# A state-space layer inside a decoder trunk: order of its stages, form of its small products, and the queue of its tables

## Chip, cores and metric

The kernel runs on one core of a Trainium2 chip. The metric is device time in microseconds (us) of one execution. The core has five engines that each work through an instruction list of their own in order: PE (matrix products), DVE and ACT (elementwise work, ACT also functions such as Gelu), POOL (elementwise work), and SP, which here only issues DMAs. POOL and ACT issue DMAs too, each from its own place in its list. An engine waits where an operand is not there yet or a buffer is still in use.

## What is computed

The reference is one step of a decoder trunk of two layers on 512 prompt tokens and 64 sample tokens, D = 1024. Each layer is `x += mixer(rmsnorm(x)); x += swiglu(rmsnorm(x))`. Layer 0's mixer is a dilated attention with a KV cache, layer 1's is an S5 state-space layer. The change is in that layer and in the setup of its tables:

```python
u = h @ w_in                                  # 64 groups of 16 channels
abar = exp(lam * dt)                          # complex, 64 states for each group
bbar = ((abar - 1.0) / lam)[..., None] * bmat
# x_t = abar * x_{t-1} + bbar u_t ;  y_t = Re(C x_t) + d_skip * u_t
g = gelu(y)
z = g @ w_glu
val, gate = split(z, 2)
return val * sigmoid(gate), h_last
```

The sample tokens are 8 rows of 8 tokens that start from given states; the prompt starts from zero.

## The kernel before

**Trunk.** Features lie on the partitions: `xT` holds 8 blocks of 128 features by 576 tokens. A large product takes float32 weights apart into a high and a low part (`split_w`: ACT writes `whi` at L99, DVE the rest `wlo` at L100), activations likewise (`xgh`, `xgl`), and adds three products, high by high, low by high and high by low, in `mm6` (L108), 288 tokens each. `fetch_w` (L85) issues a weight load on SP and, paced by a rate (`RF` by default), now and then one of the copies that shift the KV cache. PE writes to three rotating PSUM buffers `acc` 0 to 2 and a single `aux`. The order of all instructions is laid out by a scheduler from the order of the calls and the dependences; each engine then keeps its list.

**Tables.** `ssm_setup` runs in pieces during FFN 0. For each feature block f = 0..7 (128 features, 8 groups) it computes four tables and stores them to DRAM scratch: W (input to states), E (powers of the decay, one store for all f, L1291), T (input to output inside a chunk of 8 tokens, L1355) and V (states to output, four stores of 128 KB, L1369). POOL computes V (L1361 to L1366) and multiplies gt by rstd for the FFN (L1029). At the end of setup the tables of f = 0..3 are loaded back on SP (`consts`, L1096 to L1102), those of f + 4 on ACT's queue after stage 3 of f. DVE's first operation after the E store, a memset of `cb` (L1298), uses the memory from which E was stored, so it waits for that store to land.

**The norm ahead of the layer.** While FFN 0 ends, `Norm.add` for each of 8 blocks makes xgh, xgl and, for all but the first, a square on ACT (L193, into one buffer `sq`) that POOL adds to `ssum` (L194). `finish` (L199) is the product that sums it over the partitions.

**The state-space stage** (`ssm_phase`). Tokens are grouped in 64 prompt chunks and 8 sample chunks of 8 tokens, 72 columns.
- stage 1, c = 0..3: the input product of two blocks f, times the norm (L1408, DVE), to DRAM and back as `U` (128 by 8 by 72; L1409, L1413 on SP).
- stage 2, f: S = W U, 16 products of 128 rows and 64 columns (L1423); ACT copies S to `Sb` (L1425); DVE runs the recurrence over chunks (L1438 to L1447, two scans) and writes the chunk states `Xt` (L1450, L1451). Before, `Xt` has real and imaginary parts on the two halves of the partitions and one of the two half-blocks gl per slice, so that four DVE operations of 64 partitions write it; `xs0`, the sample states in that layout, is built in setup by four POOL copies (L1252).
- stage 3, f: Y = T U + V X, for each of 8 column blocks one T product (L1461) and one V product (L1462) of 128 by 128 weights; both in full float32, two records each in the trace. Gelu on ACT (L1464), to DRAM and back in token order (`yt`), split to high and low: G[f]. Y is `aux` for even f, `acc0` for odd f.
- The GLU product in 4 column blocks takes all G[f], then `Norm.add` and FFN 1 follow.

Before, the calls run as: stage 1(0), 1(1), S(0), S(1), 1(2), S(2), S(3), 1(3), stage 3(0), 3(1), S(4), S(5), 3(2), 3(3), S(6), 3(4), S(7), 3(5), 3(6), 3(7), GLU, where the scheduler moves single products between neighbours.

## Time and profile before

| what | value |
|---|---|
| median of 3 timed runs | 1497.02 us (1496.78 to 1498.91) |
| profiled execution | 1499.43 us, span 1497.7 us |
| granted clock of PE | 0.998 |
| PE busy | 1472.2 us (98% of the span) |
| DVE, ACT, POOL busy | 895.8, 527.8, 323.1 us |

In a row of groups the columns are the line, engine and operation, the names out<-in, PE's form in rows*columns (a name such as 128*64 is a weight of 128 rows and 64 columns), the shape, the count, then busy time in us and the mean of one in ns, and the idle time just before with what ended it. A timeline row starts with the start in us and the length in us; `x2` is two instructions in one row, and a note in brackets is the idle time before it and what ended it. A row of waits has the total in us, the count, and the longest. In a DMA row the last number is the median time from issue to landing.

### The profile page before, as it was taken

How to read it: one execution, taken by the hardware profiler on the slowest of the kernel's cores; microseconds unless marked ns; L12 is line 12 of the kernel's file. 1: busy time of each engine (PE TensorE's matmuls, PEld its weight loads, DVE VectorE, ACT ScalarE, POOL GpSimd, SP SyncE). 2: the span in 40 equal slices, each digit the busy share in tenths (PEclk: the TensorE clock that was granted, in tenths of full speed). 3: DMA queues.
4: the chain of work that ended last, by engine and by line, in shares of the span. 5: the costliest groups of instructions: out<-in, count | busy, mean ns of one | idle time of the engine just before them, and what ended most of it. 6: DMA issues, size and time to landing. Idle time of an engine off the chain costs nothing. (4 is left out here: it accounts for less than half of the span.)

```text
span 1497.7 us, 29564 instructions
## 1 busy us (share of the span) xinstructions
PE 1472.2 (98%) x12406; PEld 1384.5 (92%) x12406; DVE 895.8 (60%) x1507; ACT 527.8 (35%) x814; POOL 323.1 (22%) x377
## 2 busy tenths in 40 slices
PE   9999999999999999999999999999999999999998
PEld 7888777777899999999999999899999999999998
DVE  5898988745569545388687768745443323333332
ACT  4534455465552211322223453433432212221222
POOL 2022231320030174134436520201111001100100
PEclk9999999999999999999999999999999999999999
DMA  7566788989875555677867668865555655442212
GB/s 248 209 234 229 237 278 270 365 295 348 247 252 191 204 212 204 245 238 282 288 203 246 221 219 262 232 217 168 186 197 196 223 195 195 137 138 85 83 56 81
DMA packets 191861, 322.64 MB, mean 215 GB/s; under 512 B 40016, under 2 KB 138128, under 8 KB 190320
## 3 DMA queue, kind: packets, MB, share of 16 engines
q1 hardware_dynamic: 183488, 303.24, 60.0%
q10 hardware_dynamic: 5072, 10.04, 2.0%
q0 software_dynamic: 3168, 7.48, 1.5%
q8 instruction: 97, 1.59, 0.4%
q14 instruction: 36, 0.29, 0.1%
HBM read 289.22 MB, written 118.78 MB: 272 GB/s over the span
## 5 line engine op out<-in xcount | busy, mean ns | idle before, releaser
L108 PE MATMUL acc<-xgh,wlo 128*128 128x288 f32 x1760 | 377.9, 296 | 2.2 <-DVE wlo L100 2.2
L108 PE MATMUL acc<-xgh,whi 128*128 128x288 f32 x1760 | 379.1, 297 | 0.1
L108 PE MATMUL acc<-xgl,whi 128*128 128x288 f32 x1760 | 377.7, 296 | 1.0 <-DVE xgl L174 1.0
L100 DVE TENSOR_TENSOR wlo<-raw,whi 128x1024 fp32r<-128x1024 f32 (+1 forms) x166 | 214.9, 1295 | 261.9 <-ACT whi L99 258.4
L99 ACT ACTIVATE whi<-raw 128x1024 fp32r<-128x1024 f32 (+1 forms) x166 | 172.4, 1038 | 476.2 <-PE acc L108 446.0
L108 PEld LDWEIGHTS acc<-xgh,wlo 128*128 128x128 f32 x1760 | 283.2, 188 | 2.7 <-DVE wlo L100 2.5
L108 PEld LDWEIGHTS acc<-xgl,whi 128*128 128x128 f32 x1760 | 283.1, 189 | 1.5 <-DVE xgl L174 1.3
L108 PEld LDWEIGHTS acc<-xgh,whi 128*128 128x128 f32 x1760 | 282.7, 189 | 1.5 <-issue 1.0
L1029 POOL TENSOR_TENSOR gt<-gt,rstd 128x576 f32<-128x576 f32 x44 | 72.9, 1659 | 489.3 <-ACT gt L1028 489.1
L108 PE MATMUL acc<-hh,wlo 128*128 128x288 f32 x704 | 150.8, 295 | 2.1 <-DVE wlo L100 2.1
L108 PE MATMUL acc<-hh,whi 128*128 128x288 f32 x704 | 151.6, 296 | 0.0
L108 PE MATMUL acc<-hl,whi 128*128 128x288 f32 x704 | 150.9, 295 | 0.0
L340 PE MATMUL acc<-whi,xh 128*128 128x512 f32 x288 | 118.8, 414 | 0.5 <-ACT xh L280 0.4
L108 PEld LDWEIGHTS acc<-hh,wlo 128*128 128x128 f32 x704 | 112.9, 188 | 2.3 <-DVE wlo L100 2.3
L108 PEld LDWEIGHTS acc<-hh,whi 128*128 128x128 f32 x704 | 113.0, 188 | 0.6 <-issue 0.6
L108 PEld LDWEIGHTS acc<-hl,whi 128*128 128x128 f32 x704 | 113.1, 188 | 0.0
L340 PE MATMUL acc<-wlo,xh 128*128 128x512 f32 x288 | 112.2, 391 | 0.0
L340 PE MATMUL acc<-whi,xl 128*128 128x512 f32 x288 | 111.5, 393 | 0.0
L1050 DVE TENSOR_TENSOR xT<-acc,xT 128x576 f32<-128x576 f32 x48 | 36.1, 756 | 53.5 <-PE acc L108 53.5
L194 POOL TENSOR_TENSOR ssum<-ssum,sq 128x576 f32<-128x576 f32 x21 | 36.8, 1753 | 136.2 <-ACT sq L193 106.9
L340 PEld LDWEIGHTS acc<-whi,xl 128*128 128x128 f32 x288 | 54.0, 188 | 12.0
L340 PEld LDWEIGHTS acc<-whi,xh 128*128 128x128 f32 x288 | 54.0, 188 | 11.2 <-ACT xh L280 0.9
(395 smaller groups left out, 2008.5 us busy)
## 6 DMA issues: line engine op xcount, KB each, us to landing
o_kv_s<-cache_kv_w SPq DMA_DIRECT2D x64, 1020.0 KB, 6.9
kc<-cache_kv_w SPq DMA_DIRECT2D x100, 512.0 KB, 7.4
raw<-ffn_w_gate SPq DMA_DIRECT2D x44, 512.0 KB, 3.9
raw<-ffn_w_up SPq DMA_DIRECT2D x44, 512.0 KB, 3.9
raw<-ffn_w_down SPq DMA_DIRECT2D x40, 512.0 KB, 3.5
raw<-w_qkv SPq DMA_DIRECT2D x36, 512.0 KB, 7.4
kc<-qscr SPq DMA_DIRECT2D x32, 512.0 KB, 6.7
o_kv_s<-cache_kv_w SPq DMA_DIRECT2D x16, 1008.0 KB, 6.4
```

Source lines behind the costliest of these rows:

```text
L99: s.activation(hi, raw, AF.Copy)
L100: mark[0] = v.tensor_tensor(lo, raw, hi.bitcast(F32), OP.subtract)
L108: pem[0] = te.matmul(ps[:, c, :HN], w, x[:, c * HN:(c + 1) * HN], start=first and i == 0, stop=last and i == 2)
L194: g.tensor_tensor(self.ss, self.ss, sq, OP.add)
L340: ins = nc.tensor.matmul(*a, **kw)
L1029: g.tensor_tensor(t, t, nin.r, OP.mult)
L1050: v.tensor_tensor(xv, ps[m][:, :, :HN], xv, OP.add)
```

## The change

1. **Order of the stages.** `stage1` takes a function that it calls between its two halves: S(1) lies inside stage 1(2), S(3) and stage 3(0) inside stage 1(3). Stage 3 of 6 and 7 moves into the first GLU column block, whose second half goes through the k blocks with the gate and the value product side by side. S(0) uses `acc1`, stage 3(7) `aux`.
2. **Form of the products.** A T product becomes two of 64 columns. The V table and `Xt` get the recurrence's layout, [128, ri, q, chunk] with gl on the partition halves; a V product of 128 by 128 becomes four of 64 by 64 (two ri, two column halves), which add in PSUM. `Xt` is written by two DVE operations on 128 partitions, has four buffers in place of three, and takes the sample states from `x0`; `xs0` and its copies go.
3. **Tables.** V is stored by one DMA for each f; the V and E stores and all table loads are issued by POOL. `consts_in` (W, E) of f + 4 follows stage 2 of f, `consts_out` (T, V) follows stage 3.
4. `RF` goes from 0.7 to 0.72, the GLU fetches issue no cache copies, and `uP` shares its three buffers with `yt`.

```diff
-RF = 0.7
+RF = 0.72
...
+    def consts_in(f, q):
...
         q.dma_start(Ec, scn["E"][f])
+        KC[f] = [Wc, Ec]
+
+    def consts_out(f, q):
...
-        Vc = kc.tile([128, 4, 2, 128], F32, name="Vc")
-        q.dma_start(Vc, scn["V"][f].rearrange("r p q l c -> (r p) q l c"))
+        Vc = kc.tile([128, 2, 4, 128], F32, name="Vc")
+        q.dma_start(Vc, scn["V"][f])
+        KC[f] += [Tc, Vc]
...
-            for ri in range(2):
-                for gl in range(2):
-                    g.tensor_copy(xs0[ri * 64:ri * 64 + 64, gl], x0[gl * 64:gl * 64 + 64, ri])
...
-            nc.sync.dma_start(scn["E"].rearrange("f p r q c -> p r f q c"), ee.rearrange("p r (f q) c -> p r f q c", f=8))
+            g.dma_start(scn["E"].rearrange("f p r q c -> p r f q c"), ee.rearrange("p r (f q) c -> p r f q c", f=8))
...
-                for gl in range(2):
-                    for ri in range(2):
-                        nc.sync.dma_start(scn["V"][f, ri, :, :, gl, :], vv[gl * 64:gl * 64 + 64, ri].rearrange("p q c t -> p q (c t)"))
+                g.dma_start(scn["V"][f], vv.rearrange("p r q c t -> p r q (c t)"))
                 yield
-        consts(0, nc.sync)
-        consts(1, nc.sync)
+        consts(0, g)
+        consts(1, g)
     kp.append(out["es"].enter_context(L["right"]("ssmk1", bufs=2)))
-    consts(2, nc.sync)
-    consts(3, nc.sync)
+    consts(2, g)
+    consts(3, g)
...
-        for gl in range(2):
-            hs = slice(gl * 64, gl * 64 + 64)
-            v.tensor_tensor(Xt[0:64, gl, :, 1:64], ra[hs, 0], ta[hs, 0], OP.subtract)
-            v.tensor_tensor(Xt[64:128, gl, :, 1:64], ra[hs, 1], ta[hs, 1], OP.add)
+        v.tensor_tensor(Xt[:, 0, :, 1:64], ra[:, 0], ta[:, 0], OP.subtract)
+        v.tensor_tensor(Xt[:, 1, :, 1:64], ra[:, 1], ta[:, 1], OP.add)
...
-        for gl in range(2):
-            for q in range(4):
-                o = Y[:, gl, q * 72:q * 72 + 72]
-                te.matmul(o, Tc[:, 2 * q + gl, :], U[:, 2 * q + gl, :], start=True, stop=False)
-                te.matmul(o, Vc[:, q, gl, :], X[f][:, gl, q, :], start=False, stop=True)
+        for q in range(4):
+            qc = slice(q * 72, q * 72 + 72)
+            for gl in range(2):
+                for h in range(0, 128, 64):
+                    te.matmul(Y[h:h + 64, gl, qc], Tc[:, 2 * q + gl, h:h + 64], U[:, 2 * q + gl, :], start=True, stop=False)
+            for ri in range(2):
+                for gl in range(2):
+                    gs = slice(gl * 64, gl * 64 + 64)
+                    for h in range(0, 128, 64):
+                        te.matmul(Y[h:h + 64, gl, qc], Vc[gs, ri, q, h:h + 64], X[f][gs, ri, q, :], start=False, stop=ri == 1)
...
-            consts(f + 4, s)
+            consts_out(f + 4, g)
...
-    stage2(1)
-    stage1(2)
+    stage1(2, lambda: stage2(1))
     stage2(2)
-    stage2(3)
     fetch2(D)
-    stage1(3)
-    stage3(0)
+    stage1(3, lambda: (stage2(3), stage3(0)))
     stage3(1)
+    stage2(4)
     fetch2(0)
-    stage2(4)
+    stage3(2)
     stage2(5)
-    stage3(2)
     stage3(3)
     stage2(6)
     stage3(4)
     stage2(7)
-    for f in range(5, 8):
-        stage3(f)
+    stage3(5)
...
     def glu_first():
-        pg, pv = [acc(1), acc(2)], [acc(0), aux.tile([128, 2, 512], F32, name="aux")]
-        for kh in range(2):
-            for ps, c0 in ((pg, D), (pv, 0)):
-                glu_half(ps, *split_w(W2[c0][kh]), kh)
+        pg = [acc(1), acc(2)]
+        glu_half(pg, *split_w(W2[D][0]), 0)
+        stage3(6)
+        wh, wl = split_w(W2[0][0])
+        pv = []
+        for m in range(2):
+            pv.append(aux.tile([128, 2, 512], F32, name="aux") if m else acc(0))
+            for k in range(4):
+                mm6(pv[m], wh[:, k, m * 128:(m + 1) * 128], wl[:, k, m * 128:(m + 1) * 128], *G[k], k == 0, False)
+            if m == 0:
+                stage3(7)
...
+        for k in range(4):
+            for ps, wh, wl in w:
+                for m in range(2):
+                    mm6(ps[m], wh[:, k, m * 128:(m + 1) * 128], wl[:, k, m * 128:(m + 1) * 128], *G[4 + k], False, k == 3)
```

The first place is PE's list in the middle of stage 3. Before, in the stretch after stage 3(1), T (L1461) and V (L1462) products of one form alternate, with S(4) (L1423) between two blocks:

```order
L1461 MATMUL acc_10986<-U,Tc 128x72
L1462 MATMUL acc_10986<-Xt,Vc 128x72
L1423 MATMUL acc_11024<-U,Wc 64x72 x16
L1461 MATMUL aux<-U,Tc 128x72
L1462 MATMUL aux<-Xt,Vc 128x72
```

In the changed kernel PE's list has, around the same S(4) (now L1426), T (L1465) in fours and V (L1470) in eights, after the last product of stage 1(3):

```order
L108 MATMUL acc_10771<-xgh,wlo 128x288 x2
L1426 MATMUL acc_11056<-U,Wc 64x72 x16
L1465 MATMUL aux<-U,Tc 64x72 x3
L1465 MATMUL acc_10994<-U,Tc 64x72 x4
L1470 MATMUL acc_10994<-Xt,Vc 64x72 x8
```

Every T and V product now writes 64 of the partitions; T has 128 rows and V 64, so the form changes at each border between the two.

The second place is POOL's list at the end of FFN 0. Before, it holds the end of V for f = 7 (L1361 to L1366) and the adds to ssum (L194):

```order
L1363 TENSOR_TENSOR st_9894<-st_9894,vt_9895 128x512
L194 TENSOR_TENSOR ssum_5394<-ssum_5394,sq_9917 128x576
L1365 TENSOR_TENSOR vt_9895<-Cr_5478,Ai_5458 128x512
L1366 TENSOR_TENSOR st_9894<-st_9894,vt_9895 128x512
L194 TENSOR_TENSOR ssum_5394<-ssum_5394,sq_10049 128x576
L194 TENSOR_TENSOR ssum_5394<-ssum_5394,sq_10057 128x576
```

Now the same stretch of POOL's list has the V store (L1370) and the loads of the tables of f = 2 and 3 (L1095 to L1105):

```order
L1369 TENSOR_TENSOR st_9838<-st_9838,vt_9839 128x512
L1370 DMA v_scr_5040<-st_9838 128x1024
L194 TENSOR_TENSOR ssum_5394<-ssum_5394,sq_9926 128x576
L1095 DMA Wc_9899<-w_scr_5039 128x1024
L1097 DMA Ec_9901<-e_scr_5042 128x512
L1103 DMA Tc_9903<-t_scr_5041 128x1024
L1105 DMA Vc_9905<-v_scr_5040 128x1024
L1095 DMA Wc_9907<-w_scr_5039 128x1024
L1097 DMA Ec_9909<-e_scr_5042 128x512
L1103 DMA Tc_9911<-t_scr_5041 128x1024
L1105 DMA Vc_9913<-v_scr_5040 128x1024
L194 TENSOR_TENSOR ssum_5394<-ssum_5394,sq_10022 128x576
```

Eight loads, which need the memory that V's store of f = 7 reads, now stand between the first and the second add, and the first add stands behind V.

The third place is POOL's list around the end of E (the last product of its powers, and the copy of the last column). Before:

```order
L1128 TENSOR_TENSOR et_6504<-ee,U_5473 128x256
L1129 TENSOR_TENSOR ee<-et_6503,et_6504 128x32x8
L1290 COPY E_5459<-ee 128x64
L1362 TENSOR_TENSOR vt<-Cn,Ai 128x512
L1029 TENSOR_TENSOR gt<-gt,rstd 128x576 x5
```

Now, with the E store (L1294) and two E loads in the same list:

```order
L1135 TENSOR_TENSOR et_6445<-ee,U_5472 128x256
L1136 TENSOR_TENSOR ee<-et_6444,et_6445 128x32x8
L1293 COPY E_5459<-ee 128x64
L1294 DMA e_scr<-ee 256x8x256
L1365 TENSOR_TENSOR vt<-Cn,Ai 128x512
L1097 DMA Ec<-e_scr 128x512 x2
L1029 TENSOR_TENSOR gt<-gt,rstd 128x576 x4
```

The store follows the copy of E's last column in POOL's list, and the two loads stand between V's first operation and the FFN's products.

50 lines of the change are left out of this document (28 added, 22 removed).

## The prediction

> **What bounds the kernel now.** I read the page's head first, then the windows by stage, then the waits of PE inside the state-space stage, and last the timeline rows of the products that the change rewrites.
>
> ```profile
> span 1497.7 us, 29564 instructions
> 480.00:860.00 380.00, 375.66 (x2907) 372.26 (x2906) 250.19 (x439) 99.66 (x110) 163.60 (x137) 1.00 0.68 231
> 895.00:985.00 90.00, 86.78 (x865) 84.31 (x864) 67.54 (x116) 37.51 (x84) 11.27 (x19) 1.00 0.82 245
> ```
>
> In the window rows the columns after the length are the busy times of PE, PE's weight loads, DVE, ACT and POOL, then the clock and the DMA share. 480 to 860 is FFN 0 with the table setup in its gaps, 895 to 985 is the stage that the change rewrites. PE is busy in 86.78 of the 90 us there, so waits alone can give back about 3 us; anything larger has to come from PE doing the same work in less time. DVE, with 67.54 us, is the next engine. The profiled execution took 1499.43 us (span 1497.7), 2.4 us above the median of the three timed runs, 1497.02. I work out a difference on the trace and apply it to the median. A measurement of this kernel tells about 0.2% from no change, which is 3.0 us.
>
> These are all of PE's waits from 895 to 992 us:
>
> ```profile
> PE acc L108 <- DVE xgl L174: 1.0, 1, 1.0
> PE aux L1461 <- ACT ys L1464: 0.9, 2, 0.7
> PE acc L1423 <- ACT Sb L1425: 0.8, 2, 0.5
> PE aux L1462 <- issue: 0.5, 1, 0.5
> ```
>
> They add up to 3.2 us, all of them around stage 3 and the start of the GLU product.
>
> **The products of stage 3.** The rows start with the instruction's start and its length.
>
> ```profile
> 927.34 0.39 PE L1462 MATMUL aux<-Xt,Vc 128*128 128x72 f32 x2
> 927.56 0.39 PE L1461 MATMUL aux<-U,Tc 128*128 128x72 f32 x2
> 927.78 0.39 PE L1462 MATMUL aux<-Xt,Vc 128*128 128x72 f32 x2
> 928.01 0.39 PE L1461 MATMUL aux<-U,Tc 128*128 128x72 f32 x2
> ```
>
> One 128x128 product (two records, x2) starts every 0.223 us ((928.01 - 927.34) / 3). A block f has 8 T and 8 V products: 16 x 0.223 = 3.57 us. The halved T products have the form that stage 2 has already, 128 rows by 64 columns:
>
> ```profile
> L1423 PE MATMUL acc<-U,Wc 128*64 128x72 f32 x256 | 9.8, 229 | 0.8 <-ACT Sb L1425 0.8
> 911.44 0.43 PE L108 MATMUL acc<-xgh,wlo 128*128 128x288 f32 x2
> 911.80 1.22 PE L1423 MATMUL acc<-U,Wc 128*64 128x72 f32 x32
> 912.95 0.53 PE L108 MATMUL acc<-xgh,whi 128*128 128x288 f32 x2
> 913.32 0.42 PE L108 MATMUL acc<-xgl,whi 128*128 128x288 f32 x2
> 913.58 0.43 PE L108 MATMUL acc<-xgh,wlo 128*128 128x288 f32 x2
> ```
>
> Stage 2's 16 products are 32 records; from the first start to the last end they take 1.22 us, less the last one's own 0.23 us that is 0.99, so about 1.02 us with one more step. The two column halves run side by side. Sixteen halved T products per f therefore cost 1.02 us. The 32 V products of 64 rows and 64 columns have no row in the trace; the nearest are the small products of layer 0:
>
> ```profile
> 310.65 1.06 PE L760 MATMUL Sd<-kc,Pz 128*32 128x128 f32 x32
> 311.64 0.66 PE L760 MATMUL S<-kT,att 64*32 64x256 f32 x16
> 312.23 0.72 PE L760 MATMUL S<-kT,qT 64*128 64x128 f32 x8
> 312.88 1.09 PE L760 MATMUL pt<-ident,sm 128*128 128x128 f32 x8
> L760 PE MATMUL S<-kT,att 64*32 64x256 f32 x240 | 9.9, 388 | 0.0
> ```
>
> Of the 16 records of form 64*32 the last starts 0.27 us after the first (0.66 less the mean 0.388). Stage 2's step for a pair is 1.02/16 = 0.064 us at 72 columns, 0.23 us scaled to 256. So only one further group fits behind the first: eight run at once, which is both row halves and four column quarters. By that, four 64x64 products run at once: 8 groups of 2 records, 16 x 0.064 = 1.02 us per f. If the row halves did not overlap it would be 2.04. I take 1.02; the 64*32 rows have the row split in question.
>
> So T and V of one f go from 3.57 to 2.04 us, and eight of them save 8 x 1.53 = 12.2 us.
>
> **What the new forms cost.** Within stage 3 the order is now 4 T, 8 V, 4 T, 8 V and so on, and PE changes its form at each border. In the instruction order of the changed kernel I count 60 borders between 128x64 and 64x64, where before T and V had one form; the borders with full 128x128 products stay 16. What a border costs is in the rows above. From 911.44 to 911.80 are 0.36 us, where undisturbed neighbours (913.32, 913.58) are 0.26 apart: 0.10 in. After stage 2's last record (starting at 911.80 + 0.99 = 912.79) the next start is 0.16 later instead of 0.06: 0.10 out. Then the first big pair holds 0.37 instead of 0.26 us, 0.11 for loading a 128-column weight; for 64 columns I halve it, 0.05. One border between the small forms is then 0.10 + 0.05 = 0.15 us. The layer-0 rows give three more: 32 records of 128*32 come four at a time, (8 x 0.113, the step scaled to 128 columns) = 0.91 of the 0.99 to the next start: 0.08; 64*32 takes 2 x 0.23 of 0.59: 0.13; 64*128, four pairs of 0.113, takes 0.45 of 0.65: 0.20. I take 0.145, between the mean of these and the first reading, and keep 0.08 and 0.20 as ends: 60 x 0.145 = 8.7 us, from 4.8 to 12.0.
>
> The Trainium skill, "TensorEngine Tiling (Array Packing)", Tiling Modes, says that a change of mode, though not of tile, drains the TensorE: this speaks against the change and agrees with the 0.10 on either side of stage 2. The same page's Instruction Overhead, about 60 cycles for each matmul and no tiling from a dimension that is already small, would make 64 V records, estimated at 60 of the 288 columns that take 0.13 us in the input product, 0.027 us each, cost 1.8 us per f, and the forecast 6 us worse. The 16 records of form 64*32 that start within 0.27 us, 0.017 apart, speak against that here.
>
> **Waits.** S(1), S(3) and stage 3 of f = 0, 6 and 7 now lie among input or GLU products, so that there ACT's copy of S and its Gelu have products of 3.2 us and more (24 of 0.13) in front of the next user of their buffer; f = 1 to 5 still follow one another. Against it DVE has less room: its 67.54 us shrink only by the Xt writes.
>
> ```profile
> L1450 DVE TENSOR_TENSOR Xt<-R,ta 64x252 f32<-64x252 f32 x16 | 6.7, 418 | 1.2 <-PE aux L1462 0.6
> L1451 DVE TENSOR_TENSOR Xt<-R,ta 64x252 f32<-64x252 f32 x16 | 6.7, 416 | 0.2
> ```
>
> 32 of these become 16 on all partitions, of the same 252 elements: 6.7 us less, some 61 us of DVE in a stage of about 84. The recurrences have to follow one another, S(7) is followed closely by its V products, and the last xgl are wanted soon after. I leave 1.2 us of the 3.2: -2.0, with ends of -3.2 and +2.
>
> **The POOL queue at the end of FFN 0.** All table loads and the V stores now sit on POOL. Nine stores and 16 loads in FFN 0 are 25 issues more:
>
> ```profile
> L379 POOL DMA_DIRECT2D o_kv_p<-a x8 | 4.4, 556 | 15.0 <-DVE a L760 6.1 <-ACT ks L760 4.5 <-issue 2.3
> L381 POOL DMA_DIRECT2D o_kv_p<-a x8 | 4.0, 503 | 10.1 <-DVE a L760 8.1 <-issue 2.1
> ```
>
> At 0.55 us that is 14 us on an engine with 163.60 of 380 us busy; between the blocks f the wait behind them is gt x rstd (L1029), and there POOL's free time covers it. At the end it doesn't: after V of f = 7 stand one add of ssum, eight table loads that wait until that store has landed, and only then the other adds of the norm. Before, POOL had no DMA there:
>
> ```profile
> t_scr<-wo SPq DMA_DIRECT2D x3, 512.0 KB, 4.8
> 853.95 2.52 POOL L194 TENSOR_TENSOR ssum<-ssum,sq 128x576 f32<-128x576 f32 x1
> 856.50 0.69 ACT L193 ACTIVATE sq<-xT 128x576 f32<-128x576 f32 x1 [1.56 <-POOL ssum L194]
> 866.44 1.06 ACT L99 ACTIVATE whi<-raw 128x1024 fp32r<-128x1024 f32 x1 [0.71 <-PE acc L108]
> 869.70 0.43 PE L108 MATMUL acc<-xgh,whi 128*128 128x288 f32 x2
> ```
>
> The V products end 2.5 us earlier than now, since the add that lay among them (the first, as long as the second) moves behind: at 851.4. Issue 0.55, landing as the 512 KB T store 4.8: 856.8. Eight loads, 4.4: the second add starts at 861.2 instead of 853.95 and ends near 863.7. ACT is in order, and the one sq buffer makes its third square wait for that add, at 863.7 instead of 856.50. Behind it in ACT's queue are one small weight copy, two xgh, two squares (the last waits for the fourth add, about 869.3) and then the copy whi of the first input weights: 870 to 871, with wlo 1.2 us behind. PE wants whi at 869.70 and wlo two pairs (0.53) later: a stall of about 2.0 us. If the store lands in half the time nothing is lost; if it takes 9 us, 6 are. So +2.0, from 0 to +6.
>
> **The E store.** It moves from SP to POOL and DVE waits for its landing:
>
> ```profile
> 578.25 0.68 SPq L1291 DMA_DIRECT2D e_scr<-ee  x1
> 587.72 0.31 DVE L1298 MEMSET cb<- 128x128 f32 x2 [4.62 <-DMA e_scr<-ee]
> 596.56 0.53 PE L108 MATMUL acc<-xgh,wlo 128*128 128x288 f32 x2 [2.24 <-DVE wlo L100]
> ```
>
> Eight set-up operations then stand ahead of wlo on DVE, and PE stalls for 2.24 us. A landing that moves by one us moves this stall by one, down to none. POOL's issues are 0.503 us for 32 rows (L381) and 0.556 for 128 (L379), nearly flat in pieces; this store has 2048 pieces of 1 KB, so 1.6 us by that slope, 8.9 if the whole price is per piece. SP no longer queues 7 us behind the E copy, which frees the DMA engines a little earlier. I take 0, from -2.2 to +8. By the Trainium skill, "DMA: Bandwidth & Descriptors", Anatomy of one DMA, a 2 MB store from this queue takes an estimated 6.8 us, which would give back the stall; the 9.5 us between the two rows are of the other queue.
>
> **The rest, at nothing.** The four xs0 copies (POOL, in setup), the 24 fewer stores on SP and the 16 table loads taken off ACT are covered: PE's waits show none of them. The KV-cache copies (RF 0.72, none beside the GLU fetches) move between stages in which no wait of PE on a weight's DMA shows; if that cover were gone, a 512 KB weight costs at most its landing of some 5 us once.
>
> **Sum.** -12.2 + 8.7 - 2.0 + 2.0 + 0 = -3.5 us: 1497.0 - 3.5 = 1493.5.
>
> **Rivals.**
> - *The tables cost nothing* (0.24): the store lands sooner or PE has whi in time. Then -5.5, 1491.5, and down to 1488.5 with borders of 0.10. For it: POOL standing idle leaves DVE alone, whose neighbouring operations are then faster.
> - *The weave doesn't hold* (0.14): DVE is the bound inside the stage, the waits go to 3.2 + 2, so +2.0 instead of -2.0: +0.5, 1497.5, no change. For it: 67.54 us busy of 90, and a single R, Z, ta and Sb buffer; against it the 6.7 us saved.
> - *Dear borders* (0.11), slower: a border costs PE its drain and both row halves' weight loads. Sum zero at 60c = 12.2, c = 0.20; slower by over 0.2% from c = 0.25. At 0.26 it is 1500.5. The 0.20 after 64*128 speaks for it, the 0.08 and 0.13 against.
> - *The V halves run one after the other* or *POOL's long store is priced per piece* (0.08 together): +8.2 or +8, 1501.5.
> - The forecast has 0.43.
>
> **Numbers.** Faster by over 0.2% is below 1494.0: the forecast's lower 0.28, the free tables 0.24: 0.52. Within 0.2%: 0.15 of the forecast, 0.14 of the weave, 0.02 of the borders: 0.31. Slower: 0.09 + 0.08 = 0.17. The range goes from 1488.5 to 1500.5; left out are the per-piece cases and the upper tail of the borders.
>
> **What would show it.** Stage 3's T rows should come as 8 records in 0.25 us plus a border, V as 16 records in 0.25; an f in about 3.2 us (2.04 + 8 x 0.145). A V group of 0.5 us says that row halves do not overlap. POOL's wait on v_scr at the end of FFN 0, with a PE wait on wlo near 870, says that the tables cost their 2 us; no such wait, that they are free. PE's wait on wlo near 596 gives the E store. The stretch from stage 2's first product to the last one of the first GLU block should be 5 to 6 us shorter. I am wrong if it is as long as before, or if the loss sits at some other place of FFN 0.

## The result, and the profile after

The changed kernel took 1505.97 us (median of 4 runs, 1504.47 to 1508.09), beside 1497.08 us for the kernel before in the same comparison (4 runs, 1496.78 to 1498.91): a ratio of 1.0052, with an interval of 1.0038 to 1.0066. It is slower by half a per cent, where the forecast was 3.5 us faster and the range ended at 1500.5. The profiled execution took 1504.47 us (span 1502.6), 5.0 us above the profiled execution of before.

Where the time sits is read most simply from three products that occur in both kernels: the sums of squares of the three norms (L199). From the first to the second runs FFN 0, from the second to the third the state-space stage with its GLU, and behind the third the rest. PE's timeline of before, first column the start in the span:

```profile
430.93 1.13 PE L199 MATMUL aux<-ssum,ones 128*128 128x288 f32 x4
879.03 1.13 PE L199 MATMUL aux<-ssum,ones 128*128 128x288 f32 x4
1077.00 1.13 PE L199 MATMUL aux<-ssum,ones 128*128 128x288 f32 x4
```

And of after:

```profile
429.48 1.13 PE L199 MATMUL aux<-ssum,ones 128*128 128x288 f32 x4
876.22 1.13 PE L199 MATMUL aux<-ssum,ones 128*128 128x288 f32 x4
1081.82 1.13 PE L199 MATMUL aux<-ssum,ones 128*128 128x288 f32 x4
```

FFN 0 went from 448.10 to 446.74 us (-1.4), the stage with GLU from 197.97 to 205.60 (+7.6), the rest stayed (420.7 and 420.8 to the end of the span), and the attention ahead was 1.45 us shorter in this execution. The 1.4 us of FFN 0 are not a gain of the change. The execution of before that was profiled ran for a while at a lower clock behind its stall near 596, and that of after did not behind its own:

```profile
595.00:600.00 5.00, 3.44 (x18) 3.44 (x19) 4.82 (x6) 0.75 (x2) 0.00 (x0) 0.76 0.81 300
600.00:605.00 5.00, 5.00 (x36) 5.00 (x36) 1.61 (x1) 2.44 (x3) 3.69 (x2) 0.90 0.25 69
```

In these windows of before the clock is 0.76 and 0.90, which is 5 x 0.24 + 5 x 0.10 = 1.7 us lost; in after it is 1.00 throughout FFN 0. So the whole loss is in the stage that the change rewrites. This is its window in the profile of after, with the columns that the prediction explains:

```profile
895.00:985.00 90.00, 82.46 (x1312) 74.13 (x1313) 56.95 (x97) 32.31 (x77) 19.29 (x34) 0.94 0.71 213
```

Between 895 and 985 PE is busy for 82.46 us where it was 86.78, and DVE for 10.6 us less, so DVE did not become the bound. Two things are new, PE's waits and the clock, 0.94 instead of 1.00. The waits of PE from 892 to 992 us, total, times, longest:

```profile
PE acc L108 <- ACT xgh L173: 5.3, 3, 2.9
PE acc L1426 <- DMA U<-u_scr: 1.9, 2, 1.6
PE acc L1465 <- ACT ys L1472: 1.8, 1, 1.8
```

That is 9.0 us instead of 3.2. ACT, which is to make xgh from y, waits longer for y to come back from DRAM; its row from 890 to 992 us in before, and then in after:

```profile
ACT xgh L173 <- DMA yt<-y_scr: 9.3, 6, 2.6
ACT xgh L173 <- DMA yt<-y_scr: 29.2, 8, 9.5
```

In the stage the clock is at half in one stretch only:

```profile
935.00:940.00 5.00, 3.20 (x88) 2.74 (x88) 3.95 (x9) 3.05 (x10) 1.17 (x3) 0.96 0.97 342
940.00:945.00 5.00, 3.67 (x69) 2.74 (x66) 4.67 (x9) 1.61 (x7) 1.19 (x3) 0.50 1.13 319
945.00:950.00 5.00, 4.70 (x82) 4.20 (x84) 0.60 (x2) 1.11 (x3) 0.00 (x0) 0.52 0.98 285
950.00:955.00 5.00, 5.00 (x154) 4.22 (x154) 3.07 (x6) 1.31 (x4) 0.00 (x0) 1.00 0.72 186
```

Each window loses its length times what the clock lacks of 1: 0.2 + 2.5 + 2.4 = 5.1 us. So the stage can be taken apart: before, 197.97 = 3.2 of waits + 0 of clock + 194.8 of work; after, 205.60 = 9.0 + 5.1 + 191.5. The work fell by 3.3 us, and 10.9 us of waits and clock came on top. The wait of 1.63 us for U lies inside the half-clock stretch, so that up to 0.8 us of it is counted twice, and the work fell by 2.5 to 3.3 us.

The work is what the prediction said. PE's timeline of one block f in the stage, after:

```profile
918.30 0.42 PE L1465 MATMUL aux<-U,Tc 128*64 128x72 f32 x8
918.65 0.48 PE L1470 MATMUL aux<-Xt,Vc 64*64 64x72 f32 x16
...
921.09 0.48 PE L1470 MATMUL aux<-Xt,Vc 64*64 64x72 f32 x16
921.50 0.53 PE L108 MATMUL acc<-xgh,whi 128*128 128x288 f32 x2
```

The block takes 921.50 - 918.30 = 3.20 us, as forecast, where 16 of the old products took 3.57.

Where the wait of 1.8 us comes from is seen in two lists. ACT, in the profile of after:

```profile
933.58 0.68 ACT L173 ACTIVATE xgh<-yt 128x576 fp32r<-128x576 f32 x1 [3.53 <-DMA yt<-y_scr]
...
936.95 0.21 ACT L1453 ACTIVATE Zf<-Z 128x8 f32<-128x8 f32 x1 [2.48 <-DVE Z L1446]
937.07 1.05 ACT L1435 ACTIVATE tb<-zm,rho 128x64 f32<-128x64 f32 x4
938.03 0.63 ACT L1472 ACTIVATE ys<-acc 128x576 f32<-128x576 f32 x1
```

And PE at the same place:

```profile
935.68 1.22 PE L1426 MATMUL acc<-U,Wc 128*64 128x72 f32 x32
938.71 0.47 PE L1465 MATMUL acc<-U,Tc 128*64 128x72 f32 x8 [1.80 <-ACT ys L1472]
...
940.87 0.75 PE L1465 MATMUL acc<-U,Tc 128*64 128x72 f32 x8
941.55 0.76 PE L1470 MATMUL acc<-Xt,Vc 64*64 64x72 f32 x16
...
945.30 2.19 PE L1426 MATMUL acc<-U,Wc 128*64 128x72 f32 x32 [1.63 <-DMA U<-u_scr]
```

The Gelu of f = 1 (ys, at 938.03) stands in ACT's list behind the conversion xgh of f = 0, and that waits 3.53 us for y of f = 0 to come back from DRAM. Then Zf waits for DVE's recurrence, which had itself waited behind the low half of the same y. PE's T of f = 3 needs the buffer that the Gelu empties. PE stood idle from 936.9 to 938.7; from about 939.6 its clock is halved and a T group takes 0.75 instead of 0.47 us.

### The profile page after: what moved, and what is told of

It reads as the page before. It is cut to its first block, busy times and chain, and to the rows that moved or that the text cites. A ratio compares the mean times of both kernels' runs of the same rounds, so it can differ in the third digit from the quotient of the medians.

```text
span 1502.6 us, 30521 instructions
## 1 busy us (share of the span) xinstructions
PE 1472.4 (98%) x12918; PEld 1377.3 (92%) x12918; DVE 884.9 (59%) x1491; ACT 526.1 (35%) x814; POOL 331.8 (22%) x414
## 5 line engine op out<-in xcount | busy, mean ns | idle before, releaser
L100 DVE TENSOR_TENSOR wlo<-raw,whi 128x1024 fp32r<-128x1024 f32 (+1 forms) x166 | 209.7, 1263 | 233.2 <-ACT whi L99 229.2
L173 ACT ACTIVATE hh<-ut 128x576 fp32r<-128x576 f32 x44 | 30.2, 687 | 110.5 <-DVE ut L1034 110.4
L194 POOL TENSOR_TENSOR ssum<-ssum,sq 128x576 f32<-128x576 f32 x21 | 35.0, 1669 | 144.5 <-ACT sq L193 115.2
L340 PEld LDWEIGHTS acc<-whi,xh 128*128 128x128 f32 x288 | 54.0, 188 | 12.5 <-ACT xh L280 2.4
```

The lines of the kernel that those rows point to most:

```text
L100: mark[0] = v.tensor_tensor(lo, raw, hi.bitcast(F32), OP.subtract)
L173: s.activation(hi, src, AF.Copy)
L194: g.tensor_tensor(self.ss, self.ss, sq, OP.add)
L340: ins = nc.tensor.matmul(*a, **kw)
```

## The experiments

The expectations call the theories by letters. The two that carry the rest are A and B. Theory A: the DRAM round trips of u and y, with the lists of ACT, DVE and SP that must keep their order, set the pace of the stage; products that are faster no longer cover them, PE idles, and idle PE loses its clock. Theory B: the new order of the blocks alone makes the waits, whatever the products. The others are told at their runs: what the POOL queue costs (C, E), the place of the Gelu (D), the V store (F), and one set-up step fewer (H).

In the table, FFN 0 and the stage with GLU are taken from the three L199 starts as above; the waits are PE's, from 870 to 1010 us; the clock's loss is summed over windows of 5 us from 865 to 1085. A wait that falls into a half-clock stretch counts in both columns. Every row but the median and the ratio is one profiled execution. The clock's loss in FFN 0 is not in the clock column: it is 1.7 us, behind the stall near 596, in the profiles of before, order only, stage loads on ACT, late splits, after without trips and one step less, twice that in before without trips (a second stretch follows its stall near 850), and nothing in the others.

| kernel | FFN 0 | stage, GLU | waits | clock | median us (runs) | ratio to before [95%] |
|---|---|---|---|---|---|---|
| before | 448.1 | 198.0 | 3.2 | 0 | 1497.08 (4) | |
| after | 446.7 | 205.6 | 9.0 | 5.1 | 1505.97 (4) | 1.0052 [1.0038, 1.0066] |
| forms only | 443.7 | 204.3 | 9.4 | 5.1 | 1501.37 (10) | 1.0019 [1.0009, 1.003] |
| order only | 448.4 | 205.4 | 5.0 | 5.2 | 1511.14 (4) | 1.0081 [1.0057, 1.0106] |
| queues back | 443.3 | 200.8 | 5.0 | 3.4 | 1498.17 (10) | 0.9998 [0.9984, 1.0013] |
| filled | 447.9 | 209.4 | 10.3 | 5.1 | 1509.77 (6) | 1.0083 [1.0056, 1.011] |
| stage loads on ACT | 448.2 | 201.4 | 7.3 | 5.1 | 1503.99 (10) | 1.002 [1.0004, 1.0037] |
| set-up on SP | 443.5 | 205.8 | 9.5 | 6.8 | 1501.45 (10) | 1.0007 [0.999, 1.0024] |
| one V store alone | 446.5 | 211.6 | 5.5 | 13.7 | 1508.18 (10) | 1.005 [1.0033, 1.0067] |
| late splits | 449.1 | 209.1 | 13.1 | 6.9 | 1510.58 (6) | 1.0064 [1.0041, 1.0087] |
| one step less, alone | 445.9 | 200.1 | 2.5 | 3.4 | 1496.27 (8) | 0.9963 [0.9943, 0.9983] |
| T and V grouped | 443.4 | 203.5 | 12.7 | 8.5 | 1500.57 (12) | 1.0002 [0.9986, 1.0017] |
| after, no trips | 448.3 | 193.1 | 2.4 | 1.7 | 1494.02 (6) | 0.9949 [0.9929, 0.9969] |
| before, no trips | 449.3 | 195.2 | 0.7 | 0 | 1496.01 (10) | 0.996 [0.9944, 0.9976] |
| copies later | 445.2 | 198.0 | 3.3 | 0 | 1497.27 (12) | 0.999 [0.9973, 1.0006] |
| E store on SP | 445.7 | 206.3 | 8.5 | 6.8 | 1502.44 (10) | 1.0022 [1.0006, 1.0038] |

The kernel before, beside these runs, had medians of 1498.37 to 1500.02 us in its 98 executions. No run tries the new rate of the cache copies (`RF`, and none beside the GLU fetches) by itself.

**Forms only.** The changed kernel with the order of the blocks, the GLU, the queues and the buffers of before: the halved products, the states' layout and the V table are new, and with them come the single V store (here on SP) and a set-up without the xs0 copies and one empty step.

```diff
-    stage1(2, lambda: stage2(1))
+    stage2(1)
+    stage1(2)
...
-    stage1(3, lambda: (stage2(3), stage3(0)))
+    stage1(3)
+    stage3(0)
...
-                g.dma_start(scn["V"][f], vv.rearrange("p r q c t -> p r q (c t)"))
+                nc.sync.dma_start(scn["V"][f], vv.rearrange("p r q c t -> p r q (c t)"))
```

> The halved T, the 64x64 V, the recurrence's layout and the single V store, with the order of the stages, the DMA queues and the fetch rates of before. Theory A (the smaller products no longer cover the round trips of U and Y through DRAM, and the idle PE loses its clock): a stage 3 block of 3.2 us, but PE's waits in the state-space stage at 6 us or more instead of 3.2, a half-clock stretch behind one of them, and 1496 to 1503 us. Theory B (the new order of the stages makes the waits): the forms keep their gain, waits near 3 us, no half clock, 1492 to 1495 us.

Its waits of PE from 870 to 1010 us:

```profile
PE acc L1424 <- ACT Sb L1426: 4.3, 2, 3.2
PE acc L1466 <- issue: 1.6, 1, 1.6
PE aux L1466 <- issue: 1.3, 1, 1.3
PE acc L1466 <- POOL fs L1514: 1.3, 1, 1.3
PE acc L1461 <- ACT ys L1468: 0.9, 1, 0.9
```

The stage is 204.3 us, with 9.4 us of waits where before had 3.2 in the same order. Faster products make the waits without any new order, as theory A expects; that the trips are behind them this run does not show, since the profile puts them down to Sb, ys, POOL's fs and, for 2.9 us, to no releaser at all (issue). That the kernel holds to 1.0019 is owed to FFN 0, 4.4 us shorter (below).

**Order only.** The kernel before, with the changed kernel's order, GLU and buffers, and the old products.

```diff
-    stage2(1)
-    stage1(2)
+    stage1(2, lambda: stage2(1))
...
-        S = acc(2)
+        S = acc(2 if f else 1)
```

> The new order of the stages and of the first GLU block with the old 128x128 T and V products, old layout, old queues and rates. Theory A: the longer products cover the round trips as before, waits 2 to 4 us, 1495 to 1498 us. Theory B: the new order brings its waits along, 8 us or more of them with a half-clock stretch, 1501 to 1508 us.

```profile
PE acc L108 <- ACT xgh L173: 4.5, 2, 2.5
PE acc L108 <- DVE xgl L174: 0.3, 1, 0.3
PE acc L108 <- DVE wlo L100: 0.2, 1, 0.2
```

The stage is 205.4 us: 5.0 of waits, 5.2 of clock, and 195.2 of work, that of before (194.8). So B holds as well, though with fewer waits than the 8 us and a longer time than the 1501 to 1508 us that it expected. The new order starts the GLU ahead of the last two blocks, and there PE waits for xgh; with the old products the stage grows by 7.4 us, as much as by the whole change. The profile puts ACT's wait ahead of that xgh, 9.5 us, down to a table load (Vc), and not to y, so that it is the trip of y which holds it is not shown here. A and B are not rivals: each of the two edits alone makes such waits.

**Queues back.** The changed kernel, with the E and V stores and the first table loads on SP's queue and the loads of f + 4 on ACT's, as before.

```diff
-            consts_in(f + 4, g)
...
-            consts_out(f + 4, g)
+            consts_in(f + 4, s)
+            consts_out(f + 4, s)
...
-        consts(0, g)
+        consts(0, nc.sync)
```

> The changed kernel with the V and E stores and the first table loads on SP and the later ones on ACT, all of f + 4 after stage 3 of f, as before. Theory A and B: within 2 us of the changed kernel, 1503 to 1508 us. Rival C (the POOL queue delays the tables or the U loads in the stage): 1498 to 1501 us.

The ratio is 0.9998 [0.9984, 1.0013]: the whole loss is gone, and so is the gain. A and B had expected 1503 to 1508 us here, and the median of 1498.17 is that of rival C: neither carries the loss without the POOL queue. PE's wait in FFN 0 (432 to 870 us) is

```profile
PE acc L108 <- DVE wlo L100: 1.1, 1, 1.1
```

and in the stage the order on ACT has changed:

```profile
930.65 0.68 ACT L173 ACTIVATE xgh<-yt 128x576 fp32r<-128x576 f32 x1 [2.51 <-DMA yt<-y_scr]
...
931.24 0.30 ACT L1436 ACTIVATE Ss<-Sb 128x64 f32<-128x64 f32 x1
931.39 0.63 ACT L1470 ACTIVATE ys<-acc 128x576 f32<-128x576 f32 x1
934.02 0.22 ACT L1453 ACTIVATE Zf<-Z 128x8 f32<-128x8 f32 x1 [2.00 <-DVE Z L1446]
```

The Gelu of f = 1 now stands ahead of Zf, at 931.39, and PE's wait on it does not exist. Of the 5.0 us of waits that are left in this stage 4.6 are marked issue: PE stops in the middle of a group of V products, and the profile shows nothing that released it.

**Stage loads on ACT, and set-up on SP.** The two halves of the edit before, each alone. The first moves the loads of f + 4 from POOL to ACT:

```diff
-            consts_in(f + 4, g)
+            consts_in(f + 4, s)
...
-            consts_out(f + 4, g)
+            consts_out(f + 4, s)
```

> The changed kernel with only the table loads of f = 4 to 7 issued by ACT instead of POOL; V and E stores and the first loads stay on POOL. Theory D (what POOL's issuing changes in the stage is the order of ACT's list: with the loads on POOL the Gelu of f = 1 stands behind Zf and tb of S(4), with them on ACT ahead of them): PE's wait of 1.8 us on that Gelu is gone and the time is 4 to 6 us under the changed kernel, 2 to 4 us over before. Rival E (POOL costs its time only in FFN 0): the changed kernel's time, 7 to 9 us over before.

The second moves the set-up's stores and first loads from POOL to SP:

```diff
-            g.dma_start(scn["E"].rearrange("f p r q c -> p r f q c"), ee.rearrange("p r (f q) c -> p r f q c", f=8))
+            nc.sync.dma_start(scn["E"].rearrange("f p r q c -> p r f q c"), ee.rearrange("p r (f q) c -> p r f q c", f=8))
...
-    consts(2, g)
+    consts(2, nc.sync)
```

> The changed kernel with the V and E stores and the loads of f = 0 to 3 on SP; the loads of f = 4 to 7 stay on POOL. Theory D with the FFN 0 part of the queue's cost: the stretch of FFN 0 is 3 to 4 us shorter than in the changed kernel, the stage as long as there, 4 to 6 us over before. Rival E: all of the queue's 8 us come back, within 1 us of before.

With "after" and "queues back" these make a square, and the two effects stay apart in it. With the stage's loads on POOL the stage takes 205.6 and 205.8 us, with them on ACT 201.4 and 200.8: 4.2 to 5.1 us. With the set-up on POOL FFN 0 takes 446.7 and 448.2 us, on SP 443.5 and 443.3. Of the 448.2 us 1.7 are half clock, which the other three do not have; without it both differences are 3.2 to 3.3 us. The set-up on SP still has the stage's waits on xgh, U and ys (4.5, 2.8 and 1.7 us). The timed ratios come in this order, 1.0052 with both on POOL, 1.002 and 1.0007 with one, 0.9998 with none, but the last two can't be told apart, so that with the set-up on SP the stage's 5.1 us stand in the profiles only. For rival E, which puts all of the queue's cost into FFN 0, speaks that time; against it speak the profiles and the time of "stage loads on ACT", 4.0 us over before where E expected 7 to 9.

**E store on SP.** The E store alone goes back to SP; the V stores and all loads stay on POOL.

```diff
-            g.dma_start(scn["E"].rearrange("f p r q c -> p r f q c"), ee.rearrange("p r (f q) c -> p r f q c", f=8))
+            nc.sync.dma_start(scn["E"].rearrange("f p r q c -> p r f q c"), ee.rearrange("p r (f q) c -> p r f q c", f=8))
```

> The changed kernel with the E store alone back on SP; the V stores and all table loads stay on POOL. If the E store is the queue's cost in FFN 0: the wait near 596 us falls from 2.7 to 1.1 us, FFN 0 at 443 to 445 us and 2 to 4 us under the changed kernel. If the table loads between POOL's products are: the wait falls but FFN 0 stays over 446 us because of PE's small waits near 700 us. The stage stays at 205 us or more in either case.

PE's wait on wlo near 596 fell from 2.7 to 1.7 us and FFN 0 from 446.7 to 445.7, both without a loss of clock: the store's queue is worth 1.0 us of the 3.3. All waits of PE in FFN 0 are 3.7 us in the changed kernel, 2.6 here and 1.1 with the set-up on SP. Among the 2.6 is the small wait of 0.6 us on hl near 700, which neither kernel with its set-up on SP has, so waits account for 1.5 of the remaining 2.3 us, and POOL's other issues between the FFN's products for some of them; the rest is open. The stage kept its 206.3 us, and the interval of the ratio overlaps that of "set-up on SP".

**Filled.** Sixteen more products of 72 columns, whose results nobody reads, eight behind S(5) and eight behind stage 3(3), where PE idles:

```diff
+    def warm(n, f):
+        D_ = acc(1)
+        for i in range(n):
+            te.matmul(D_[:, 0, :72], KC[f][0][:, 0, 0, :], Uc[f][:, 0, :], start=True, stop=True)
...
     stage2(5)
+    warm(8, 5)
     stage3(3)
+    warm(8, 5)
```

> The changed kernel with 16 added products of 128x128 by 72 columns (8 behind S(5), 8 behind stage 3 of 3) into an unused PSUM buffer, 1.8 us of PE work in each of the two waits around the half-clock stretch. They compute nothing that is used. If the idle PE is what halves its clock: granted clock 1.00 between 930 and 955 us, and 3 to 7 us less than the changed kernel, 1499 to 1503 us, though work is added. If the small products themselves are what halves it: the clock stays at half there and the time is the changed kernel's or up to 4 us more, 1505 to 1510 us.

From 930 to 955 us the clock is 1.00, but the stage grew to 209.4 us, and PE's largest wait is a new one of 6.5 us on Sb, followed by half clock from 960 to 967. (The profiled execution took 1517.19 us, 7.4 above the median.) The filling used a buffer and a place in PE's list of its own and moved the wait instead of covering it, so it does not tell the idle time from the clock.

**Late splits.** Each y's load and conversion (L1475 to L1478) is moved to a later place of the program, so that no Gelu stands behind the wait for y:

```diff
-        yt = wk.tile([128, NT], F32, name="yt", bufs=3)
-        nc.sync.dma_start(yt, scn["Y"][f])
         if f < 4:
             consts_out(f + 4, g)
+
+    def join(f):
+        yt = wk.tile([128, NT], F32, name="yt", bufs=3)
+        nc.sync.dma_start(yt, scn["Y"][f])
         G[f] = L["split"](xg, yt, None, "xgh", "xgl")
...
     stage2(5)
+    join(0)
     stage3(3)
```

> The changed kernel, all tables on POOL, with the reload of y and its split into high and low called later: that of f = 0 behind S(5), and so on, the last ones behind stage 3 of 7. Then the Gelu of f = 1 stands ahead of Zf and tb in ACT's list. Theory D: the wait of 1.8 us and the half clock behind it are gone, 3 to 6 us under the changed kernel. Rival G (the table loads themselves, issued early by POOL, hold up the loads of U and y): the waits come at other places and the time stays within 2 us of the changed kernel.

The wait on ys is gone, as theory D wanted; in its place PE waits 7.3 us on Sb and 4.2 on xgh, and the kernel is at 1.0064, no better than the changed one, where D expected 3 to 6 us less (the profiled execution took 1513.93 us, 3.4 above the median). So moving that Gelu forward did not get its wait back. The edit also asks for every y later, so it does not show what the Gelu's place alone is worth.

**T and V grouped.** The kernel "queues back", with all T products of a block ahead of all V products, which takes away six of the seven borders inside a block.

```diff
-                    te.matmul(Y[h:h + 64, gl, qc], Tc[:, 2 * q + gl, h:h + 64], U[:, 2 * q + gl, :], start=True, stop=False)
+                    te.matmul(Y[h:h + 64, gl, qc], Tc[:, 2 * q + gl, h:h + 64], U[:, 2 * q + gl, :], start=q == 0, stop=False, skip_group_check=True)
+        for q in range(4):
+            qc = slice(q * 72, q * 72 + 72)
```

> The changed kernel with the tables on SP and ACT as before (as in the run with the queues back) and, in each stage 3, all 16 T products ahead of all 32 V products: 2 borders of form for each f instead of 8, some 45 fewer, 6.5 us of PE work by 0.145 us each. Theory A (the stage is set by the round trips and lists, not by PE): waits grow by about as much, the time stays within 2 us of the run with the queues back, that is of before. Rival (PE's work still counts in full): 5 to 7 us under before.

PE's timeline of its block f = 0:

```profile
916.25 1.17 PE L1463 MATMUL aux<-U,Tc 128*64 128x72 f32 x32
917.35 1.23 PE L1470 MATMUL aux<-Xt,Vc 64*64 64x72 f32 x64
918.51 0.54 PE L108 MATMUL acc<-xgh,whi 128*128 128x288 f32 x2
```

A block takes 918.51 - 916.25 = 2.26 us instead of 3.20. Eight of them are 7.5 us less for PE, and the kernel is not faster: 1.0002 [0.9986, 1.0017] beside 0.9998 [0.9984, 1.0013] with the borders. Its waits in the stage:

```profile
PE acc L108 <- ACT xgh L173: 4.3, 3, 2.0
PE acc L1426 <- ACT Sb L1428: 4.0, 2, 2.4
PE acc L1426 <- DMA U<-u_scr: 3.3, 1, 3.3
...
```

12.7 us of waits instead of 5.0, and 8.5 of clock instead of 3.4. PE's work is not what the stage lasts, as theory A has it; what does hold the stage of the changed kernel is shown by the next two runs.

**No trips, after and before.** Both kernels with u written straight into U and y converted from ys, without the four DMAs of each block; what is left out is the exchange of layout between partitions and columns.

```diff
-            u = wk.tile([128, 2, HN], F32, name="yt", bufs=3)
-            v.tensor_tensor(u, ps[m][:, :, :HN], nin.r, OP.mult)
-            nc.sync.dma_start(scn["U"][f], u.rearrange("p h x -> p (h x)"))
...
+            v.tensor_tensor(U.rearrange("p a b -> p (a b)").rearrange("p (h x) -> p h x", h=2), ps[m][:, :, :HN], nin.r, OP.mult)
...
-        nc.sync.dma_start(dram(scn["Y"], f * 128 * NT, [[72, 128], [9216, 8], [1, 72]]), ys.rearrange("p q l c -> p (q l) c"))
...
-        G[f] = L["split"](xg, yt, None, "xgh", "xgl")
+        G[f] = L["split"](xg, ys.rearrange("p q l c -> p (q l c)"), None, "xgh", "xgl")
```

> The changed kernel without the round trips of U and Y through DRAM: U and the input of the split are read in SBUF as they are written, so that the tokens and channels are not regrouped and the state-space layer computes on the wrong layout; every product, ACT and DVE operation stays. Theory A: PE's waits in the stage fall under 2 us, no half clock there, from the norm of the layer to the next norm 191 to 195 us instead of 205.6, and 4 to 9 us under before. Rival (the waits come from DVE and ACT themselves): 5 us or more of waits stay, and the time is over before.

> Before without the round trips of U and Y through DRAM, in the same way (wrong layout, all operations). Theory A: from norm to norm 195 to 197 us instead of 198.0, 1 to 3 us under before, since there the trips were nearly covered; the same leave-out in the changed kernel saves three times as much or more. Rival: it saves as much here as there.

All waits of PE in the stage of the changed kernel without trips:

```profile
PE acc L1421 <- ACT Sb L1423: 2.4, 2, 2.2
```

and of the kernel before without them:

```profile
PE aux L1457 <- issue: 0.7, 1, 0.7
```

The trips are worth 12.5 us of the stage to the changed kernel (205.6 to 193.1) and 2.8 to the one before (198.0 to 195.2). Before, the products hid them; after, they don't. (Of the changed kernel's waits 2.4 us on Sb stay, with 1.7 us of clock.) The four DMAs leave SP's queue too, so the two runs show what the trips cost as a whole, and not how much of it is their landing and how much their place in SP's list. Without them the changed kernel's stage is the shorter one by 2.1 us, in one profile each; timed, 0.9949 [0.9929, 0.9969] and 0.996 [0.9944, 0.9976] overlap.

**One V store alone.** The kernel before, with the V table stored in one piece, and its two halves sorted by four loads for each f (on SP, and for f + 4 on ACT's queue) instead of by four stores.

```diff
-                for gl in range(2):
-                    for ri in range(2):
-                        nc.sync.dma_start(scn["V"][f, ri, :, :, gl, :], vv[gl * 64:gl * 64 + 64, ri].rearrange("p q c t -> p q (c t)"))
+                nc.sync.dma_start(scn["V"][f], vv.rearrange("p r q c t -> p r q (c t)"))
...
-        q.dma_start(Vc, scn["V"][f].rearrange("r p q l c -> (r p) q l c"))
+        for r in range(2):
+            for l in range(2):
+                q.dma_start(Vc[r * 64:r * 64 + 64, :, l, :], scn["V"][f, l * 64:l * 64 + 64, r])
```

> Before with one change: V goes to DRAM in one store on SP for each f instead of four of 128 KB, in the layout of the change, and is loaded by four pieces of 64 partitions, so that the tile in SBUF, the products and their order are those of before. Theory F (the V stores on SP are what made FFN 0 4 to 5 us shorter in the runs with a single store on SP): 3 to 5 us under before. Rival (the removed xs0 copies or the layout did it): within 1 us of before.

FFN 0 kept both stalls of 2.1 us, so theory F, that the stores made them, falls; the 446.5 us are those of before, 448.1, less the 1.7 us of clock. The stage took 211.6 us with twelve more issues in ACT's list, 5.5 us of waits and 13.7 us of clock, 12 of them in one stretch that begins in the wait of 2.9 us on ys; that the issues are the cause was not tried.

**One step less, alone.** The kernel before, with one line taken out: an empty step of the set-up, behind the copies of x0, which the change had dropped with them.

```diff
-            yield
             yield
```

> Before with one empty step of the table setup left out (one of the two yields behind the xs0 copies, which the change drops with them); the copies themselves stay. FFN 0 was 4.4 to 4.8 us shorter in the three kernels of the change that have their setup on SP, and no shorter with the single V store alone. Theory H (the table setup comes one step earlier against FFN 0, so that its pieces no longer meet the norm at the end): FFN 0 at 443 to 445 us instead of 448.1 and 3 to 5 us under before. Rival (the four xs0 copies on POOL did it): FFN 0 and the time as before, within 1 us.

PE's waits in FFN 0 (432 to 870 us):

```profile
PE acc L108 <- DVE wlo L100: 2.2, 1, 2.2
```

Of the two stalls of 2.2 and 2.1 us the second is gone, FFN 0 is 2.2 us shorter with the same 1.7 us of clock in both, and the kernel stands at 0.9963 [0.9943, 0.9983]: faster than the one before, and than the changed one at 1.0052. It has the lowest median of the kernels that do the whole work. Of its 5.5 us by the ratio (0.0037 x 1500; 3.5 between the medians) the trace shows the 2.2; the profiled execution lost 3.4 us of clock in the stage and was no shorter than before's (span 1498.6), and the run after this one puts the gain lower.

**Copies later.** The same, and the four copies of xs0 on POOL moved behind the E store, to see whether they are what still separates 445.9 from the 443.4 of the kernels with the states' new layout.

```diff
-            for ri in range(2):
-                for gl in range(2):
-                    g.tensor_copy(xs0[ri * 64:ri * 64 + 64, gl], x0[gl * 64:gl * 64 + 64, ri])
             yield
...
+            for ri in range(2):
+                for gl in range(2):
+                    g.tensor_copy(xs0[ri * 64:ri * 64 + 64, gl], x0[gl * 64:gl * 64 + 64, ri])
```

> Before with the empty step left out and the four xs0 copies moved on POOL from ahead of the powers of E to behind the E store. Theory H (both the step and POOL's 3.2 us ahead of E count): the E store is issued some 3 us sooner and PE's wait on wlo near 596 us falls from 2.2 to about 1.1, FFN 0 at 443 to 444 us, 6 to 8 us under before and 1 to 3 under the run with the step alone. Rival (the copies had slack): as the run with the step alone.

FFN 0 took 445.2 us with two waits, 2.4 and 0.4, and the time can't be told from the kernel before (0.999 [0.9973, 1.0006]), although it lacks the same step. The two runs together leave the step's gain at some 1 to 5 us by time. Without the clock's loss the three FFN 0 are 446.4 (before), 444.2 (one step less) and 445.2 us. The copies are not shown to be the cause; why the E stall is 1.1 us in "queues back" and 2.2 to 2.4 in these two stays open.

## Why the prediction was wrong

The profile's two differences, -1.4 in FFN 0 and +7.6 in the stage, are set against the sum of -3.5. The step that failed is that of the waits, with the clock behind them: they were to fall by 2.0 us and rose by 5.8, and half clock took 5.1 more. Beside it the POOL queue, taken at nothing in the stage and at +2.0 at the end of FFN 0, cost 8.2 us in the two together, none of it at that place. The timed difference, 8.9 us, is larger than the profiles' 5.0, because before's profiled execution lies 2.4 us above its median and the changed kernel's 1.5 below its own; against the medians of before beside the experiments (1498.37 to 1500.02) it would be 6.0 to 7.6 us.

- *The products (-12.2).* Right. In "T and V grouped" 16 T products with their border take 1.10 us and 32 V products 1.16; four 64x64 products do run at once. The rival that the halves run one after the other fell. The 1.16 us are also below the 1.7 us (1.8 in the prediction) that 64 records would take at the 0.027 us each that the prediction estimated from the Trainium skill, "TensorEngine Tiling (Array Packing)", Instruction Overhead.
- *The borders (+8.7).* Right. 3.20 less 2.26 us for six borders is 0.157 each; 0.145 was taken. The two terms together were forecast at -3.5; the work of the stage fell by 2.5 to 3.3. (With borders of 0.10 the first rival's sum is 1488.8 and not 1488.5.)
- *The waits ("I leave 1.2 us of the 3.2").* This step failed, and it takes the most from the forecast. The waits went to 9.0 us, 5.8 up instead of 2.0 down. I looked at which products stand in front of the next user of a PSUM buffer and at DVE's sum of busy time, and weighed nothing for the u and y trips. Their landings were in the trace of before (medians of 4.6 and 5.2 us for u out and back, 5.1 and 3.2 for y), as was the fact that ACT, DVE and SP keep their order. What a faster PE would ask for earlier was not asked. Without the trips the same kernel's stage is 12.5 us shorter, and that of before 2.8. The rival "the weave doesn't hold" had the right place and the wrong engine and size: +2.0, by DVE as the bound, while DVE's load fell to 56.95 us of 90.
- *The clock.* The sum had no term for it. It lost 5.1 us in this profile, in one stretch that begins 0.8 us after the wait of 1.8 us ends and has the wait of 1.63 us in it.
- *The POOL queue at the end of FFN 0 (+2.0).* Wrong in place. POOL's timeline after:

```profile
844.07 0.59 POOL L1370 DMA_DIRECT2D v_scr<-st  x1 [0.30 <-POOL st L1369]
844.68 1.61 POOL L194 TENSOR_TENSOR ssum<-ssum,sq 128x576 f32<-128x576 f32 x1
847.55 0.56 POOL L1095 DMA_DIRECT2D Wc<-w_scr  x1 [1.25 <-PE acc L108]
...
851.27 0.53 POOL L1105 DMA_DIRECT2D Vc<-v_scr  x1
851.82 1.44 POOL L194 TENSOR_TENSOR ssum<-ssum,sq 128x576 f32<-128x576 f32 x1
```

The eight loads took 0.53 to 0.56 us each, as taken, but they began at 847.55 and not at 856.8. The V store went out at 844.07 instead of 851.4: the set-up has one step less, so all of V sits one gap of FFN 0 earlier ("one step less" shows it by itself: POOL's last product of V ends at 845.5 there, and at 854.0 in before). I had listed the dropped line and followed nothing that it moved. PE waited for nothing there, and the stall of 2.1 us that before had at 850.95 went with it.
- *The E store (0, from -2.2 to +8).* Inside its bounds. POOL's timeline after:

```profile
576.68 1.35 POOL L1294 DMA_DIRECT2D e_scr<-ee  x1
```

And its row of the DMA issues, with the time to landing last:

```profile
e_scr<-ee POOLq DMA_DIRECT2D x1, 2048.0 KB, 10.1
```

Its issue of 1.35 us is near the 1.6 of the flat slope, and it landed 10.1 us later, not the 6.8 that was estimated by the Trainium skill, "DMA: Bandwidth & Descriptors", Anatomy of one DMA; the measurement decides. PE's stall near 596 became 2.7 us, and 1.7 with the store back on SP.
- *"The 16 table loads taken off ACT are covered."* Failed. On POOL they cost the stage 4.2 to 5.1 us in the profiles. With them gone from ACT's list the Gelu of f = 1 came to stand behind Zf, but "late splits" undid that and won nothing, so how they cost it is not settled. The set-up's issues on POOL cost FFN 0 another 3.2 to 3.3 us. Both were taken at nothing because PE's waits of before do not show them, which is true of any operation that does not yet stand in that list.
- *FFN 0's own gain.* Not foreseen at all: with the old queues it is 443.3 to 443.7 us instead of 448.1 (forms only, queues back, set-up on SP, grouped). Of these 4.4 to 4.8 us 1.7 are the half clock of before's own execution and 2.2 the dropped step; the last 0.5 to 0.9 are not settled.

So in the profiles the change is four parts that mostly cancel: in "queues back" less work in the stage (-2.4) and a shorter FFN 0 (-4.8, of which 1.7 are before's clock) against 5.2 us more of waits and clock; and 8.2 us for the POOL queue on top (FFN 0 and stage of after, 652.3, less those of "queues back", 644.1). Together they are the +6.2 of the two profiles. That the round trips make the waits is shown for the changed kernel by the run without them; for "queues back", with 4.6 us of its waits marked issue, it is not.

## What to carry to other kernels

An engine that is 96% busy still covers round trips of others; before making its work shorter, list what it will ask for earlier (each DMA trip, and each list that waits on it in order) and price that from the trace's landings. A DMA issue is an operation in a list: moving it to an idle queue changes what stands behind what on both, and a step dropped from an interleaved set-up moves every later step. Where an edit takes work away, allow for a loss of clock behind each new idle stretch, look for such a loss in the profile of before as well, and time the parts alone: here the best of them, at 0.9963, was one dropped line.

## What the runs showed of the hardware

- Half clock comes in stretches of about 3.4 us or a few of them. "Queues back" lost 3.4 us in two stretches, which is 1.7 each; after lost 5.1 us in one of 10.2 us. By the Trainium skill, "TensorE: Matmul & The Clock Gate", Part 1, the gate judges a free-running window of some 3.4 us, halves the rate after an idle one and restores it after a busy one. The length agrees. What does not follow from it is that a wait of 1.80 us was enough here, and that the clock stayed low for 10.2 us though PE, from 939.52 to 943.67, ran 72-column products without a gap.
- An idle stretch is no sure price: "copies later" had waits of 2.4 us in FFN 0 and up to 1.0 us in the stage and lost no clock in either, and in the profile of after the stall of 2.7 us that ends at 595.66 and the wait of 2.92 us that ends at 961.58 cost none, while the stall of 2.24 us in before cost 1.7. Over before's 98 executions the 11 with a granted clock of 0.993 or less have a median of 1505.3 us, the 32 at 0.999 or 1.000 one of 1498.6: a good part of what looks like noise between runs of one kernel goes with the clock (a straight line through clock and time takes the standard deviation from 2.7 to 1.8 us).
- Splitting a product into two of half the rows costs PE next to nothing in itself: 64 records of 64*64 took 1.16 us and 32 of 128*64 1.10, each with one border. The price sits at the border between two forms, 0.157 us.
